# Thirty-six unread products in front, earlier weights, split runs of small products and a later modulation in a diffusion layer

## The chip, the cores and the metric

The kernel runs on one core of a Trainium2 chip. The metric is the device time of one execution in microseconds (us). Before the change three runs gave 960.75, 961.24 and 962.13 us; the median is 961.24 us.

## The reference

One layer of a hybrid diffusion model over 512 latent tokens and 256 context tokens, width 1024. All arithmetic is float32.

```python
mod = silu(c) @ w_ada + b_ada; mod_c = silu(c_ctx) @ w_ada + b_ada
sh1, sc1, gt1, sh2, sc2, gt2 = split(mod, 6)
h  = rms_norm(x, g_norm1) * (1 + sc1) + sh1
hc = rms_norm(ctx, g_norm1) * (1 + csc1) + csh1
aq, ak, av, dq, dk, dv, dz, da, db, ga, gd = split_cols(h @ w_in)      # and the same of hc
y_attn = window_ctx_attention(q_a, k_a, v_a, k_ac, v_ac, attn_sink)
o_dc, s_cf, s_cb = bidir_delta(context, zero states)    # chunks of 64 tokens, two directions
o_dl, _, _       = bidir_delta(latents, s_cf, s_cb)
y = sigmoid(ga) * (y_attn @ w_br_attn) + sigmoid(gd) * (y_d @ w_br_dn)
x = x + gt1 * (y @ w_out)
x = x + gt2 * (square(relu((rms_norm(x, g_norm2) * (1 + sc2) + sh2) @ w_mlp1)) @ w_mlp2)
```

The delta rule is computed in chunks of 64 tokens: in each chunk a triangular system is inverted, and a scan over the chunks carries a 64 x 64 state for each head and direction.

## The kernel before

**Layout.** Features lie on the 128 partitions and tokens on the free axis. Every large product is made as three passes of rounded float32: weights and activations are each split into a high and a low part (`hi`, `lo`), and `mm3` (L266 to L273) issues high x high (L271), high x low (L272) and low x high (L273). A weight block of 128 x 1024 (512 KB) is fetched by `wload` (L255 to L264): one DMA on the queue of SyncE into one of four buffers `wr`, then ACT writes the high part (L262) and VectorE (DVE) the low part (L263).

**Order.** The Python program writes the work in the order of priority. The framework then puts each engine's instructions into one fixed order from its own model of the times; on the chip each engine takes its own instructions in that order. Generators are woven by counts: `weave` advances several of them in proportion to step numbers, and `run_fill(n)` issues the next n of 432 products of 128 x 512 (L970 and L925: the attention branch's projection and the gate tiles) which serve as filling wherever a serial chain would leave TensorE (PE) waiting. `FILL` and the counts beside it set how many go where.

**Front (0 to 65 us).** SyncE issues x (four transfers of 512 KB), two blocks of `wada1`, the context (two transfers), then further blocks of `wada1`. `ada(kt)` (L190 to L201) multiplies the condition by its block of `w_ada` (L198), `columns(kt, ...)` (L209 to L222) turns the result into two columns of scale and shift (L212, L217, L220, L221). The sum of squares is built by ACT (L236) and DVE (L240, L244) and summed over partitions by a product with ones (L247). `modulate` (L275 to L279) makes the high and low part of one of eight blocks of h (L276, L277, L278). As each block becomes ready, three tiles of the input projection whose accumulators stay open in PSUM, the `early` ones, get that block's products: the decay and beta columns (`T_AB`) and the first two key tiles (`T_DK`, `T_DK + 1`). Their weights are loaded inside the loop over the blocks, two at block 0 and one at block 1.

**Middle (98 to 160 us).** `chunk_mats` (L687 to L726) builds the chunk matrices of three groups of four chunks. It begins with `half_products` (L675 to L685), one unbroken run of 128 small float32 products of 64 x 32 by 64 x 32; each takes two PE instructions of its own and two weight loads (256 matmuls and 256 loads in all, L684). It is woven with the attention's input tiles, 16 steps against 32. DVE then forms the matrices (L700, L712, L714, L721, L722), PE sums the decays (L701, L702).

**Late stage (376 to 433 us).** After the context's scan, `combine` (L768 to L800) forms the lower block of the inverse for each of the two latent groups: 64 small products (L776, L777), a copy by ACT (L778), 64 small products (L785, L786). Then, again for each group, `half_products` with q (L684), DVE multiplies with the decays (L1160, L1161) and ACT places the copies (L1168 to L1170). Ahead of each go `run_fill(28)` or `run_fill(36)` and `run_late(6)` or `run_late(3)`.

**Late modulation.** `late_mod` (L984 to L994) computes the remaining four groups of modulation columns without PE: for each of 32 blocks a DMA of 512 KB into a buffer of the same four `wr` buffers (L988), then one DVE instruction that multiplies and sums (L990). 24 of the 32 are issued by `run_late`; the last 8 are issued in the MLP.

**Second scan (431 to 511 us).** Eight steps of both directions, each step in three parts with a chain PE (L1036), DVE (L1040, L1041), PE (L1048), DVE (L1054), PE (L1067), DVE (L1078), and the outputs (L1085, L1090, L1093). Between the parts stand 8, 7 and 3 filling products. What is left of the 24 late blocks follows the scan.

**End.** The branch projection, the output projection (`mm3` with `residual`, L1253 and L1257, 24 products a tile), the norm, and the MLP.

## Time and profile before

The profile is of one execution on the chip. That execution took 959.5 us as the device counts it; its span, from the first instruction to the last, is 957.7 us.

| | |
|---|---|
| median of three runs | 961.24 us |
| profiled execution | 959.5 us |
| its span | 957.7 us |
| granted TensorE clock, mean | 0.979 |
| PE busy | 905.8 us, 95% |
| DVE busy | 596.6 us, 62% |
| ACT busy | 444.7 us, 46% |

PE is the matmul unit of TensorE, PEld its weight loads, DVE VectorE, ACT ScalarE, POOL GpSimd, SP SyncE (SPq is SyncE's queue, which issues the DMAs). The page gives busy times, the span in 40 slices (in tenths, with the granted PE clock in its own row), the DMA queues, the chain that ended last and the costliest groups of instructions. Further views are asked of the trace: waits (who waited for whom), windows (busy time, granted clock and DMA share in chosen stretches), lines (groups by source line) and a timeline. A busy PE is not a PE at its peak, because matmuls overlap; the spacing of starts says more.

### The profile page before, as it was taken

To read this page: it belongs to the slowest core of one execution; us is meant where nothing else is said; L and a number is where in the kernel's file an instruction comes from. 1 tells how busy PE (TensorE), PEld (TensorE's weight loads), DVE (VectorE), ACT (ScalarE), POOL (GpSimd) and SP (SyncE) were. 2 spreads that over 40 slices of the span, in tenths; PEclk is the share of its full clock that TensorE was granted. 3 is DMA by queue.
4 is the path that set the end of the run, shared out by engine and by line. 5 is a ranking of instruction groups with operands and counts; after the bars stand their busy time and mean duration, and the time that the engine had idled before them with its cause. 6 is when DMAs were issued, how large, how long until landed. Compare 5 with 4: busy or idle time off the path is not lost. (4 is left out here: it accounts for less than half of the span.)

```text
span 957.7 us, 18080 instructions
## 1 busy us (share of the span) xinstructions
PE 905.8 (95%) x7696; PEld 731.6 (76%) x7696; DVE 596.6 (62%) x994; ACT 444.7 (46%) x815; POOL 36.4 (4%) x45
## 2 busy tenths in 40 slices
PE   3999889999899999879999999999999999999998
PEld 1688667877677677658787879988888888888886
DVE  4666778997788899755577665982365225423511
ACT  5357634337567877337555433661154115313400
POOL 0001211000000000100011000000000000000000
PEclk9799989999999999889999999999999999999999
DMA  9721102110001133850123534381164213322101
GB/s 357 297 95 44 46 25 66 67 45 24 11 13 34 34 100 107 300 202 25 46 69 122 187 132 154 120 278 65 42 206 137 78 66 131 111 66 74 59 34 54
DMA packets 29601, 98.72 MB, mean 103 GB/s; under 512 B 3664, under 2 KB 4176, under 8 KB 29520
## 3 DMA queue, kind: packets, MB, share of 16 engines
q1 hardware_dynamic: 29520, 97.57, 29.6%
q8 instruction: 60, 0.98, 0.4%
q14 instruction: 21, 0.17, 0.0%
HBM read 95.46 MB, written 2.10 MB: 102 GB/s over the span
## 5 line engine op out<-in xcount | busy, mean ns | idle before, releaser
L271 PE MATMUL banks<-m,m 128*128 128x512 f32 (+1 forms) x584 | 219.8, 380 | 1.3 <-ACT m L277 1.3
L272 PE MATMUL banks<-m,m 128*128 128x512 f32 (+1 forms) x584 | 219.8, 378 | 0.0
L273 PE MATMUL banks<-m,m 128*128 128x512 f32 (+1 forms) x584 | 218.7, 378 | 0.8 <-DVE m L263 0.8
L262 ACT ACTIVATE m<-wr 128x1024 fp32r<-128x1024 f32 x67 | 71.1, 1062 | 149.8 <-PE banks L272 78.0
L271 PEld LDWEIGHTS banks<-m,m 128*128 128x128 f32 x584 | 109.7, 189 | 23.4 <-issue 3.1
L273 PEld LDWEIGHTS banks<-m,m 128*128 128x128 f32 x584 | 109.7, 189 | 22.0 <-DVE m L263 1.1
L272 PEld LDWEIGHTS banks<-m,m 128*128 128x128 f32 x584 | 110.1, 189 | 21.0 <-issue 0.8
L263 DVE TENSOR_TENSOR m<-wr,m 128x1024 fp32r<-128x1024 f32 x67 | 82.0, 1224 | 63.9 <-ACT m L262 34.8
L271 PE MATMUL banks<-m,wh 128*128 128x512 f32 (+1 forms) x312 | 114.3, 367 | 0.4 <-DVE m L537 0.4
L272 PE MATMUL banks<-m,wh 128*128 128x512 f32 (+1 forms) x312 | 112.2, 360 | 0.0
L273 PE MATMUL banks<-m,wl 128*128 128x512 f32 (+1 forms) x312 | 111.8, 359 | 0.0
L925 PE MATMUL banks<-m,wh 128*128 128x512 f32 x320 | 108.2, 413 | 0.0
L1352 DVE SCALAR_TENSOR_TENSOR m<-banks,modT,m 128x512 f32<-128x512 f32 x32 | 24.0, 750 | 104.0 <-PE banks L273 104.0
L262 ACT ACTIVATE wh<-wr 128x1024 fp32r<-128x1024 f32 (+1 forms) x60 | 56.6, 944 | 56.1 <-PE banks L272 23.9
L263 DVE TENSOR_TENSOR wl<-wr,wh 128x1024 fp32r<-128x1024 f32 (+1 forms) x60 | 64.7, 1078 | 22.6 <-ACT wh L262 22.3
L925 PEld LDWEIGHTS banks<-m,wh 128*128 128x128 f32 x320 | 61.7, 196 | 13.7
L925 PE MATMUL banks<-m,wl 128*128 128x512 f32 x160 | 67.3, 421 | 0.0
L271 PEld LDWEIGHTS banks<-m,wh 128*128 128x128 f32 x312 | 59.0, 189 | 9.5 <-DVE m L537 0.7
L272 PEld LDWEIGHTS banks<-m,wh 128*128 128x128 f32 x312 | 59.3, 190 | 9.0 <-issue 0.5
L273 PEld LDWEIGHTS banks<-m,wl 128*128 128x128 f32 x312 | 59.0, 189 | 8.7 <-DVE wl L263 0.3
L179 ACT ACTIVATE m<-m 128x512 fp32r<-128x512 f32 (+1 forms) x56 | 35.0, 630 | 47.5 <-DVE m L1335 19.9
L180 DVE TENSOR_TENSOR m<-m,m 128x512 fp32r<-128x512 f32 (+1 forms) x56 | 38.2, 689 | 20.9 <-ACT m L179 20.4
(229 smaller groups left out, 1293.3 us busy)
## 6 DMA issues: line engine op xcount, KB each, us to landing
wr<-in_wm SPq DMA_DIRECT2D x64, 512.0 KB, 3.5
wr<-in_win SPq DMA_DIRECT2D x39, 512.0 KB, 3.6
wa<-in_wada SPq DMA_DIRECT2D x32, 512.0 KB, 4.3
m<-in_wada SPq DMA_DIRECT2D x16, 512.0 KB, 10.2
m<-in_xT SPq DMA_DIRECT2D x8, 512.0 KB, 6.0
wr<-in_wbr SPq DMA_DIRECT2D x16, 256.0 KB, 2.7
wr<-in_wout SPq DMA_DIRECT2D x8, 512.0 KB, 3.7
out<-m SPq DMA_DIRECT2D x8, 256.0 KB, 2.0
```

Of the source, the lines that this page charges most:

```text
L179: A.activation(r32(hi), src, AF.Copy)
L180: (eng or V).tensor_tensor(r32(lo), src, hi, op=ALU.subtract)
L262: A.activation(r32(hi), raw, AF.Copy)
L263: V.tensor_tensor(r32(lo), raw, hi, op=ALU.subtract)
L271: PE.matmul(acc, w[0][:, k, :], xhi, start=(start and i == 0), stop=False)
L272: PE.matmul(acc, w[0][:, k, :], xlo, start=False, stop=False)
L273: PE.matmul(acc, w[1][:, k, :], xhi, start=False, stop=(stop and i == n - 1))
L925: PE.matmul(acc.ap, w[x][:, k, :], hx[k][y], start=(k == p == 0), stop=(k == KT - 1 and p == 2))
L1352: V.scalar_tensor_tensor(xn_[ct], acc.ap, modT[:, 3, ct:ct + 1], xn_[ct], op0=ALU.mult, op1=ALU.add)
```

## The change

1. 36 products of the 128 x 128 tile of ones with itself are issued on PE ahead of everything else; nothing reads them.
2. `wload` is defined earlier, and the three early weights are loaded one each: after the context's transfers, after block 1's `ada`, and in the first pass of the loop over blocks. The second key tile now takes part from block 0.
3. `half_products` yields after its first half. In the middle stage each half is followed by steps of the other work (`HPAUSE = 2`, the step count of the weave is 22 in place of 16). In the late stage 12 of the filling products that stood ahead of it are issued between the halves (`FPAUSE`). `combine` gets a call between its two runs, which issues 12 of the products that stood ahead of it (`CPAUSE`).
4. The 24 late blocks leave the late stage: one is issued after the second and one after the third part of each step of the second scan (16), the other 8 by twos in the first four tiles of the output projection.

```diff
+NONES = 36
 AHEAD = 2
-LATE = 6, 3, 0
+LATE = 1
+HPAUSE = 2
+FPAUSE, CPAUSE = 12, 12
...
+    wb_ = banks.get(512, True)
+    for _ in range(NONES):
+        PE.matmul(wb_[:, :P], ones, ones, start=True, stop=True)
+    wb_.free()
...
+    early, EARLY = [], {T_AB: 0, T_DK: 0, T_DK + 1: 0}
+    ebufs = []
+
+    def load_early():
+        bb = alloc(1024), alloc(1024)
+        ebufs.extend(bb)
+        early.append((wload(I["win"][list(EARLY)[len(early)]], bufs=bb), bank(2)))
+
     columns(0, ada(0))
     for k4 in range(KT // 4):
         nc.sync.dma_start(out=cs_[:, k4 * 1024:(k4 + 1) * 1024], in_=I["ctxT"][k4])
+    load_early()
...
-    early, EARLY = [], {T_AB: 0, T_DK: 0, T_DK + 1: 1}
-    ebufs = []
     for kt in range(1, AHEAD):
         columns(kt, ada(kt))
+        load_early()
...
-        for t_, k0 in EARLY.items():
-            if k0 == kt:
-                bb = alloc(1024), alloc(1024)
-                ebufs += bb
-                early.append((wload(I["win"][t_], bufs=bb), bank(2)))
+        if len(early) < len(EARLY):
+            load_early()
...
         for i in range(16):
+            if i == 8:
+                yield
...
-        half_products(kD, kO, gi, kT)
+        for _ in half_products(kD, kO, gi, kT):
+            for _ in range(HPAUSE):
+                yield
...
         A.activation(Ys.ap, Y.ap, AF.Copy)
         Y.free()
+        between()
         XO = bank()
...
-    weave((mats(), 16), (att, ATT))
+    weave((mats(), 16 + 3 * HPAUSE), (att, ATT))
...
-        run_fill(FILL[1])
-        run_late(LATE[0])
-        combine(NTO[1 + g], f[:, :, :HC], xr3[0][:, ms], b[:, :, :HC], xr3[1][:, ms], f, b, True)
+        run_fill(FILL[1] - CPAUSE)
+        combine(NTO[1 + g], f[:, :, :HC], xr3[0][:, ms], b[:, :, :HC], xr3[1][:, ms], f, b, True, lambda: run_fill(CPAUSE))
...
-        run_fill(FILL[2])
-        run_late(LATE[1])
+        run_fill(FILL[2] - FPAUSE)
         qD, qO = bank(), bank()
-        half_products(qD, qO, 1 + g, qT)
+        for _ in half_products(qD, qO, 1 + g, qT):
+            run_fill(FPAUSE)
...
         run_fill(FILL[3][n % 3])
-        if n % 3 == 2:
-            run_late(LATE[2])
+        if n % 3:
+            run_late(LATE)
     for _ in fill:
         pass
-    run_late(24)
...
         mm3(acc.ap, w, ys)
+        run_late(2)
         residual(ct, acc, slice(0, 512))
         acc.free()
+    run_late(24)
```

More of the change, by code (lines that the diff above doesn't have):

```diff
@@ L222, in columns, with wload @@
         mp_.free()
+    def wload(src, n=KT, bufs=None):
+        raw = sb.tile([P, KT, P], F32, tag="wr", bufs=NWR, name=nm("wr"))[:, :n]
+        nc.sync.dma_start(out=raw, in_=src)
+        if bufs:
+            hi, lo = (b.ap.rearrange("p (k c) -> p k c", k=KT) for b in bufs)
+        else:
+            hi, lo = (sb.tile([P, KT, P], F32, tag=t, bufs=NWS, name=nm(t))[:, :n] for t in ("wh", "wl"))
+        A.activation(r32(hi), raw, AF.Copy)
+        V.tensor_tensor(r32(lo), raw, hi, op=ALU.subtract)
+        return r32(hi), r32(lo)
+    early, EARLY = [], {T_AB: 0, T_DK: 0, T_DK + 1: 0}
[4 more added lines that the diff above has]
+        early.append((wload(I["win"][list(EARLY)[len(early)]], bufs=bb), bank(2)))
     columns(0, ada(0))
@@ L252, in tile_layer @@
         act(r, r, AF.Exp, scale=-0.5)
-    def wload(src, n=KT, bufs=None):
-        raw = sb.tile([P, KT, P], F32, tag="wr", bufs=NWR, name=nm("wr"))[:, :n]
-        nc.sync.dma_start(out=raw, in_=src)
-        if bufs:
-            hi, lo = (b.ap.rearrange("p (k c) -> p k c", k=KT) for b in bufs)
-        else:
-            hi, lo = (sb.tile([P, KT, P], F32, tag=t, bufs=NWS, name=nm(t))[:, :n] for t in ("wh", "wl"))
-        A.activation(r32(hi), raw, AF.Copy)
-        V.tensor_tensor(r32(lo), raw, hi, op=ALU.subtract)
-        return r32(hi), r32(lo)
     def mm3(acc, w, xs, start=True, stop=True, ks=None):
@@ L766, in back, with combine @@
         V.transpose(dst.rearrange("p m i -> p i m"), X3[g].rearrange("p r s -> p s r") if swap else X3[g])
-    def combine(nto, XTf, XRf, XTb, XRb, XAf, XAb, inplace):
+    def combine(nto, XTf, XRf, XTb, XRb, XAf, XAb, inplace, between=lambda: None):
         Y, Ys = bank(), alloc(512)
```

## The prediction

> **What bounds the kernel now.** I read the page first.

> ```profile
> span 957.7 us, 18080 instructions
> ...
> PE 905.8 (95%) x7696; PEld 731.6 (76%) x7696; DVE 596.6 (62%) x994; ACT 444.7 (46%) x815; POOL 36.4 (4%) x45
> ...
> DVE  4666778997788899755577665982365225423511
> ...
> PEclk9799989999999999889999999999999999999999
> ...
> q8 instruction: 60, 0.98, 0.4%
> ```

> PE bounds it: 95% busy, no other engine over 62%. In the row PEclk (40 slices of 24 us, tenths of the full clock) the granted clock drops in the second slice, in the sixth and in the seventeenth and eighteenth. So I asked the waits of PE, then a table of stretches (us; busy time and count of PE, PEld, DVE, ACT, POOL; granted clock; DMA share; GB/s).

> ```profile
> PE banks L684 <- issue: 11.3, 5, 3.4
> PE banks L198 <- DMA m<-in_wada: 11.1, 1, 11.1
> PE banks L785 <- issue: 3.6, 2, 2.0
> ...
> PE banks L1048 <- DVE m L1041: 0.9, 1, 0.9
> ```

> ```profile
> 11.10:20.10 9.00, 5.85 (x38) 1.89 (x38) 4.16 (x7) 3.61 (x6) 0.00 (x0) 1.00 1.03 411
> 20.10:33.70 13.60, 11.03 (x47) 7.01 (x48) 9.83 (x19) 6.60 (x12) 0.00 (x0) 0.50 1.03 410
> ...
> 98.30:136.40 38.10, 30.32 (x843) 22.41 (x841) 31.95 (x46) 20.04 (x35) 10.22 (x7) 0.91 0.13 44
> 380.70:431.00 50.30, 40.17 (x1127) 32.25 (x1126) 31.77 (x52) 18.95 (x29) 5.18 (x10) 0.85 0.72 252
> 441.80:451.60 9.80, 9.80 (x179) 8.03 (x178) 5.76 (x13) 6.64 (x27) 0.00 (x0) 1.00 0.16 57
> ```

> The longest waits of PE are for nothing that the profile shows (issue: 11.3 + 3.6 us), all in the runs of small products, and for the first block of `w_ada`. The clock is at 0.50 from 20 to 34 us, 0.91 in the middle and 0.85 in the late stage. The change touches just these stretches, and the second scan, where PE is full.

> **Front.** Twelve transfers of 512 KB stand ahead of the first early weight in SyncE's queue; with the change eight do. At 410 GB/s one takes 512 KB / 410 = 1.28 us, so it lands 5.1 us sooner; block 1 of `w_ada` lands 1.3 us later, block 2 2.6, block 3 1.3, the rest when they did. The rows are start, length, engine, line.

> ```profile
> 17.75 1.07 PE L198 MATMUL banks<-m,m 128*32 128x256 f32 x16 [0.57 <-DVE modS L221]
> 19.97 0.72 ACT L277 ACTIVATE m<-m,modS 128x512 fp32r<-128x512 f32 x1 [1.44 <-DVE m L276]
> 23.02 1.94 PE L198 MATMUL banks<-m,m 128*32 128x256 f32 x16
> 25.68 1.04 ACT L262 ACTIVATE m<-wr 128x1024 fp32r<-128x1024 f32 x1
> 26.77 0.79 PE L271 MATMUL banks<-m,m 128*128 128x512 f32 x1
> 64.68 0.40 PE L271 MATMUL banks<-m,wh 128*128 128x512 f32 x1
> ```

> ```profile
> L271 PE MATMUL banks<-m,m 128*128 128x512 f32 (+1 forms) x48 | 17.9, 377 | 0.0
> L198 PE MATMUL banks<-m,m 128*32 128x256 f32 x80 | 6.2, 412 | 0.0
> L217 PE MATMUL banks<-c_prm,m 128*128 128x2 f32 x21 | 2.9, 236 | 0.0
> ...
> 421.12 0.63 PE L925 MATMUL banks<-m,wh 128*128 128x512 f32 x2
> 421.81 0.63 PE L925 MATMUL banks<-m,wh 128*128 128x512 f32 x2
> ```

> Block 0's high part is there at 19.97 + 0.72 = 20.7 us, but the first early product starts at 26.77, behind the split of its weight (25.68 + 1.04). Three full products take 421.81 - 421.12 = 0.69 us, so 0.23 each, and one of half width is put at 0.117. From 26.77 to 64.68 PE does three lines of 48 (half of them full, half of half width: 72 x 0.23 + 72 x 0.117 = 25.0 us), five blocks of L198 (1.07 each at full clock: 5.4) and L217 (2.9): 33.3 us in 37.9. The rest is the 0.50 clock up to 33.7 and gaps.

> With the weight 5.1 us sooner the first early product can follow block 0's high part, at 20.0 (a little sooner than 20.7, as the same block of L198 takes 1.94 us at half clock and 1.07 at full). Block 2's `ada` is then still to do (1.6 us with L217). I add 2.5 us of gaps, since until 25 us weights and columns come one transfer at a time: 20.0 + 33.3 + 1.6 + 2.5 = 57.4, 7.3 us sooner, if the clock is granted from 20 us on. Two of its steps (3.4 us each) at half would cost 3.4. I take 6.5 us, range 3 to 9.

> ```profile
> 242.09 1.05 PE L536 MATMUL banks<-c_ident,st 128*128 128x128 f32 x8
> ```

> The 36 products cost nothing: four of their shape take 1.05 us, so 36 some 9 at full clock, 13 with the first 5 us at half; PE waits for `w_ada` until 11.1 us anyway. If they end at 12.5, the block's first products slip by 1.4 us, and the L247 behind them waits until 12.98 in any case. Their use is the clock. Before, it fell at 20.1 us though PE was busy 5.85 of the 9 us before, so the ones alone may not hold it to the first early product. [...] Hence 6.5, not 7.3.

> **Middle.**

> ```profile
> 100.27 1.67 PE L684 MATMUL banks<-m 64*32 64x32 f32 x175
> 104.03 0.73 PE L684 MATMUL banks<-m 64*32 64x32 f32 x61 [2.08 <-issue]
> 128.87 1.14 PE L684 MATMUL banks<-m 64*32 64x32 f32 x82 [2.38 <-DVE m L714]
> 416.13 1.05 PE L925 MATMUL banks<-m,wh 128*128 128x512 f32 x2
> 417.41 1.05 PE L925 MATMUL banks<-m,wh 128*128 128x512 f32 x2
> ```

> A run of 256 matmuls and 256 loads goes at about 9.5 ns a pair (1.67 / 175), then stops. The page has 60 instruction transfers of 0.98 MB in all, 16 KB each; 2 x 7696 PE instructions over 60 are 256 to a transfer. [...]

> ```profile
> L684 PE MATMUL banks<-m,m 64*32 64x32 f32 x512 | 5.5, 200 | 6.4 <-issue 6.4
> ...
> L925 PE MATMUL banks<-m,wh 128*128 128x512 f32 x68 | 24.9, 449 | 0.0
> L925 PE MATMUL banks<-m,wl 128*128 128x512 f32 x33 | 15.3, 464 | 0.0
> ```

> What a pause must be: these rows are of the late stage; its two unbroken runs of L684 stop for 6.4 us, 3.2 each. So a pause of some 3.2 us in the middle of a run hides its stop. The split puts about three attention steps of three products (0.69 us or more each) between the halves, 2.1 us, and a half itself is no longer than one block; I leave 0.3 us a run, up to 1.1. Issue stops here are 11.3 - 6.4 = 4.9 us. The clock at 0.91 of 38.1 us is 0.09 x 38.1 x 2 = 6.9 us at half, and the next step lies in the 136s: some three steps of 3.4 us. In one, three products take 417.41 - 416.13 = 1.28 us against 0.69, so a step loses 1.6; three lose about 4.1, as the middle one ran small products. Together 9.0 us.

> Not all of it comes back: DVE is busy 31.95 of 38.10 us here, so it becomes the bound once PE gains 6.2 us, and the 2.38 us wait for L714 with its clock step is DVE's already. [...] I take 5.5 us, range 2 to 9.

> **Late stage.** The stretch of 50.3 us holds 101 filling products (68 + 33 in the rows above, 23.2 us), four runs of `combine` of 128 pairs (9.5 ns each, 1.2 us), two of L684 (2.4 us) and eight changes of shape at 0.3: 35.2 us. The 15.1 us left are four stops (6.4 + 3.6 = 10.0) and the clock of 0.85, which by 0.15 x 50.3 is up to 7.5 us of lost clock, part of it under stops. The change moves no PE work out of this stretch; it puts 12 products (2.8 us, and 0.3 of switching) into each of the four places, 3.1 us against the 3.2 needed. I leave 0.3 a stop, 0.6 for two more switches and 0.5 for a chain that now shows: 15.1 - 1.2 - 0.6 - 0.5 = 12.8 us. [...] The removed 18 late blocks free DVE, for which PE did not wait here. Range 8 to 15.

> **Second scan and output projection.**

> ```profile
> DVE m L990 <- DMA wa<-in_wada: 11.4, 9, 4.0
> ...
> L990 DVE SCALAR_TENSOR_TENSOR m<-wa,m x32: 1214/1222/1496, 380.0 to 632.1; 128x1024 f32<-128x1024 f32 x32
> ...
> 442.11 1.23 DVE L263 TENSOR_TENSOR wl<-wr,wh 128x1024 fp32r<-128x1024 f32 x1 [0.20 <-ACT wh L262]
> 443.25 0.68 DVE L930 SCALAR_TENSOR_TENSOR m<-m,m 128x512 f32<-128x512 f32 x1
> 443.85 0.75 DVE L1040 TENSOR_TENSOR m<-banks,eg 128x256 f32<-128x256 f32 x2
> 445.86 1.15 PE L1048 MATMUL banks<-m,m 64*64 64x64 f32 x32
> ```

> A late block is put at 1.3 us of DVE (1222 ns and a short read of the sum). Two a step are 2.6 us in steps of 9.8 us, of which DVE works 5.76: 8.4, still under. Behind each waits the chain (L1040, L1054, L1078), and behind that PE with its next part. Here 1.9 us of L263 and L930 stood ahead of L1040, and L1048 still started in time. So a late block fits a gap as a rule; I put 0.1 us on each of 16, 1.6 us, and take back the one wait of L1048 for L1041 (0.9), which late blocks at the scan's end now cause: 0.7 lost. Bounds: 0.9 gained; 16 x 1.3 = 21 lost with no cover. The moved DMAs share SyncE's queue and the four `wr` buffers with the gate weights, 2 + 18/24 = 2.75 transfers a step on 4 buffers: over one step of lead. The other 8 blocks, two to a tile of 24 products (5.5 us), add 2.6 us to a DVE that the page has at 5 or 6 tenths in slices 24 and 25: just under full, and PE needs DVE only once a tile; 0, at most 3.

> **Sum.** 6.5 + 5.5 + 12.8 - 0.7 = 24.1 us off the execution of 959.5 us (span 957.7 and 1.8 around it). The median is 1.7 above that execution, so I forecast 961.2 - 24.1 = 937.1 us.

> **Rivals.**
> - A, the forecast, 0.64.
> - B, the front gives 1 us or nothing: ACT's fixed order still splits the first weight late, or block 1 and 2, now later, hold PE up. For it: DVE busy 9.83 of 13.60 us there. Against: the weight's split moves ahead in the program. 943 to 944 us; 0.15.
> - C, the stops are not a matter of fetched instructions, and halves change nothing (or the pauses are too short by far): front 6.5 less switches and scan, 957. [...] 0.07.
> - D, late blocks lie on the scan's chain without cover: 20 us given back, 956. Against: the 1.9 us above. 0.06.
> - E, slower: DVE meets late blocks whose transfer has not landed, as it did nine times for 11.4 us before (1.3 each, 4.0 at most), and everything behind waits. 16 x (1.3 + 1.3) = 41.6, less 25.7: 977 us. It decides from 1.6 us a block on. Against: one to 4.9 us here, where before nine waits came at one to 2 us. 0.05.
> - That nothing moves as written, or gains and losses cancel: 0.03.

> **The numbers.** B's 944 and the ends of A (3 + 2 + 8 less 3 of scan and projection: 951; 9 + 9 + 15 and 0.9: 927) give 927 to 951; C, D, E and the last lie outside, 0.2. Faster by over 0.2% (1.9 us, what a measurement tells here): A, B, C, D, 0.92; within: 0.03; slower: 0.05.

> **What would show it.** Right: PE busy from 1 us; clock 1.00 at 20 to 34 us; first early product near 20 us, first `wh` product near 58; issue waits of L684 and L785 under 3 us together; no 0.50 in the late stage, which shrinks from 50 to about 37 us; scan steps still under 10 us. Wrong: stops as long with a pause before them; L1048 or L1067 waiting for DVE by over 0.3 us a step; DVE waiting for `wa` in the scan.

## The result and the profile after

The changed kernel takes 948.87 us, the median of four runs (946.67, 946.76, 950.98 and 952.39), beside 961.0 us before. The ratio is 0.9875, with a 95% interval of 0.9837 to 0.9913. The gain is 12.1 us where 24.1 were forecast: inside the range, at half the size.

The profiled execution is the one of 950.98 us, with a span of 949.2 us. Its page first, then the waits of PE (us in total, times, longest).

```profile
span 949.2 us, 18234 instructions
...
PE 915.3 (96%) x7768; PEld 738.1 (78%) x7768; DVE 596.2 (63%) x994; ACT 444.6 (47%) x815; POOL 37.4 (4%) x45
...
PEclk8899999999999999999999999999999999999999
```

```profile
PE banks L394 <- ACT m L391: 4.1, 2, 2.4
PE banks L289 <- ACT m L240: 3.4, 1, 3.4
PE banks L700 <- issue: 3.0, 2, 2.0
...
PE banks L1055 <- issue: 2.2, 1, 2.2
```

The lines have moved: the half products are L700 (L684 before), `mm3` is L289 to L291, the first part of a scan step is L1055 (L1036), a late block L1009 (L990), the filling products L944 (L925), the split of a weight L240 and L241. The 11.1 us wait for `w_ada` is filled by the ones, which count as busy. The issue waits fell from 14.9 us to 5.2 (3.0 + 2.2), but one of them stands at a place where none stood, and ACT is new in the list.

The stretches that answer to those before (us; busy time and count of PE, PEld, DVE, ACT, POOL; granted clock; DMA share; GB/s), and the second scan of before for comparison:

```profile
15.51:18.93 3.42, 0.16 (x2) 0.07 (x1) 2.64 (x5) 3.42 (x5) 0.00 (x0) 1.00 1.02 406
18.93:32.58 13.65, 12.98 (x54) 6.33 (x54) 6.62 (x12) 5.00 (x10) 0.00 (x0) 0.50 1.03 410
96.40:136.40 40.00, 34.60 (x863) 25.63 (x861) 34.10 (x46) 20.84 (x36) 9.27 (x6) 0.91 0.14 42
378.70:417.50 38.80, 37.93 (x1137) 30.11 (x1136) 15.55 (x20) 23.32 (x40) 5.19 (x10) 1.00 0.29 91
417.50:500.40 82.90, 78.41 (x1397) 63.19 (x1389) 58.74 (x125) 48.13 (x154) 7.06 (x8) 1.00 0.41 129
```

```profile
431.00:510.30 79.30, 78.42 (x1395) 63.91 (x1389) 49.34 (x106) 50.06 (x162) 6.27 (x8) 0.99 0.19 61
```

The clock is at 0.50 for as long as before (13.65 us), only 1.1 us sooner. The late stage is what was hoped: 38.8 us in place of 50.3, without a stop and at full clock. The scan is 3.6 us longer with the same PE work.

All kernels are cut here at the same five places by the starts of PE's instructions (us): the first `wh` product, the first transpose of the attention's outputs, the first product of `combine` for the latent groups, the start of the second scan, its last output.

| kernel | to first `wh` | middle | outputs, first scan | late stage | second scan | rest | median | ratio to before, 95% |
|---|---|---|---|---|---|---|---|---|
| before | 64.7 | 135.0 | 181.0 | 50.3 | 79.3 | 447.4 | 961.0 | |
| changed | 64.6 | 131.9 | 182.1 | 38.8 | 82.9 | 448.8 | 948.9 | 0.9837 to 0.9913 |
| late_alone | 64.8 | 135.0 | 182.4 | 46.1 | 80.3 | 447.6 | 955.5 | 0.9938 to 0.9969 |
| blocks_back | 62.1 | 131.9 | 180.5 | 46.1 | 82.1 | 447.3 | 949.4 | 0.9869 to 0.9911 |
| no_pause | 63.6 | 132.0 | 182.3 | 42.1 | 84.9 | 449.2 | 956.0 | 0.9928 to 0.9971 |
| mid_whole | 64.5 | 130.9 | 177.9 | 38.7 | 84.7 | 448.5 | 948.5 | 0.9864 to 0.9903 |
| clock_held | 62.2 | 132.1 | 179.3 | 38.7 | 81.8 | 448.4 | 943.7 | 0.9808 to 0.9843 |
| mid_quarters | 62.1 | 137.8 | 178.7 | 38.7 | 81.1 | 447.9 | 948.5 | 0.9853 to 0.9901 |
| held_8_after_scan | 63.1 | 132.1 | 179.2 | 39.3 | 80.8 | 447.8 | 944.0 | 0.9804 to 0.9855 |
| no_ones | 62.8 | 132.9 | 177.7 | 39.9 | 83.0 | 449.1 | 944.3 | 0.9817 to 0.9871 |
| held_no_ones | 62.2 | 134.5 | 177.7 | 39.3 | 85.4 | 447.9 | 949.5 | 0.9866 to 0.9927 |
| held_more | 61.6 | 132.0 | 184.9 | 38.7 | 81.2 | 448.7 | 946.7 | 0.9830 to 0.9892 |
| ones_alone | 64.1 | 130.9 | 183.3 | 44.6 | 84.3 | 447.3 | 957.1 | 0.9944 to 0.9987 |
| shift40 | 63.6 | 132.0 | 178.0 | 39.0 | 81.2 | 449.5 | 945.1 | 0.9814 to 0.9870 |

Stretches are of one execution, medians of four to twelve. The column of the outputs and the first scan, which no kernel edits, varies from 177.7 to 184.9 us: a difference of that size is no effect of an edit by itself. The front varies too: PE's order up to the first `wh` product is one and the same in the changed kernel, blocks_back, no_pause and mid_whole, and that product comes at 64.6, 62.1, 63.6 and 64.5 us.

### The profile page after: what moved, and what is told of

Same layout as the page of the kernel before. It is cut to its first block, busy times and chain, and to the rows that moved or that the text cites. A ratio compares the mean times of both kernels' runs of the same rounds, so it can differ in the third digit from the quotient of the medians.

```text
span 949.2 us, 18234 instructions
## 1 busy us (share of the span) xinstructions
PE 915.3 (96%) x7768; PEld 738.1 (78%) x7768; DVE 596.2 (63%) x994; ACT 444.6 (47%) x815; POOL 37.4 (4%) x45
## 5 line engine op out<-in xcount | busy, mean ns | idle before, releaser
L289 PE MATMUL banks<-m,m 128*128 128x512 f32 (+1 forms) x584 | 220.3, 380 | 3.8 <-ACT m L240 3.4
L290 PE MATMUL banks<-m,m 128*128 128x512 f32 (+1 forms) x584 | 220.3, 379 | 0.2 <-DVE m L183 0.2
L291 PE MATMUL banks<-m,m 128*128 128x512 f32 (+1 forms) x584 | 220.1, 378 | 0.0
L240 ACT ACTIVATE m<-wr 128x1024 fp32r<-128x1024 f32 x67 | 70.9, 1062 | 153.9 <-PE banks L290 91.9
L289 PEld LDWEIGHTS banks<-m,m 128*128 128x128 f32 x584 | 109.8, 189 | 26.9 <-ACT m L240 3.4
L241 DVE TENSOR_TENSOR m<-wr,m 128x1024 fp32r<-128x1024 f32 x67 | 81.8, 1224 | 75.4 <-ACT m L240 39.3
L291 PEld LDWEIGHTS banks<-m,m 128*128 128x128 f32 x584 | 109.8, 189 | 21.9 <-issue 1.2
L289 PE MATMUL banks<-m,wh 128*128 128x512 f32 (+1 forms) x312 | 114.1, 367 | 1.3 <-DVE m L1270 0.8
L291 PE MATMUL banks<-m,wl 128*128 128x512 f32 (+1 forms) x312 | 112.2, 360 | 0.3 <-DVE wl L241 0.3
L944 PE MATMUL banks<-m,wh 128*128 128x512 f32 x320 | 105.4, 402 | 0.0
L241 DVE TENSOR_TENSOR wl<-wr,wh 128x1024 fp32r<-128x1024 f32 (+1 forms) x60 | 64.6, 1077 | 36.0 <-ACT wh L240 35.5
L240 ACT ACTIVATE wh<-wr 128x1024 fp32r<-128x1024 f32 (+1 forms) x60 | 56.5, 943 | 32.6 <-PE banks L290 17.6
L944 PEld LDWEIGHTS banks<-m,wh 128*128 128x128 f32 x320 | 59.3, 188 | 12.8
L289 PEld LDWEIGHTS banks<-m,wh 128*128 128x128 f32 x312 | 59.2, 190 | 10.9 <-DVE m L1270 1.0
L290 PEld LDWEIGHTS banks<-m,wh 128*128 128x128 f32 x312 | 59.3, 190 | 9.0 <-issue 0.5
L291 PEld LDWEIGHTS banks<-m,wl 128*128 128x128 f32 x312 | 59.1, 190 | 9.0 <-DVE wl L241 0.8
L944 PE MATMUL banks<-m,wl 128*128 128x512 f32 x160 | 65.6, 410 | 0.3 <-DVE wl L241 0.3
L182 ACT ACTIVATE m<-m 128x512 fp32r<-128x512 f32 (+1 forms) x56 | 35.2, 631 | 47.6 <-DVE m L1354 21.1
L183 DVE TENSOR_TENSOR m<-m,m 128x512 fp32r<-128x512 f32 (+1 forms) x56 | 38.4, 688 | 20.7 <-ACT m L182 20.2
```

The source lines that it names most:

```text
L182: A.activation(r32(hi), src, AF.Copy)
L183: (eng or V).tensor_tensor(r32(lo), src, hi, op=ALU.subtract)
L240: A.activation(r32(hi), raw, AF.Copy)
L241: V.tensor_tensor(r32(lo), raw, hi, op=ALU.subtract)
L289: PE.matmul(acc, w[0][:, k, :], xhi, start=(start and i == 0), stop=False)
L290: PE.matmul(acc, w[0][:, k, :], xlo, start=False, stop=False)
```

## The experiments

### The late stage: pauses, and blocks

**late_alone**: the kernel before with the late stage's pauses alone.

```diff
-        run_fill(FILL[1])
+        run_fill(FILL[1] - CPAUSE)
...
-        run_fill(FILL[2])
+        run_fill(FILL[2] - FPAUSE)
...
-        half_products(qD, qO, 1 + g, qT)
+        for _ in half_products(qD, qO, 1 + g, qT):
+            run_fill(FPAUSE)
```

> The kernel before with the late stage's pauses alone: the runs of combine and of the q products are cut in the middle by 12 filling products taken from those ahead of them; ones, early weights, middle and late modulation stay as before. Theory (the late stage's gain is fetched instructions hidden behind a pause): the stage between the first run of combine for the latent groups and the scan shrinks by 11 to 12 us as it did in the changed kernel (50.3 to 38.8), L684 and L785 lose their 10 us of issue waits there, and the median falls by 10 to 11 us, to 950 to 951, less about 2 us if the scan's first run now stops. Rival (the gain needs the late blocks gone from this stage): it stays above 44 us and the median above 955.

The stage took 46.1 us, the median was 955.5: the theory fell, the rival holds. The stops are nearly gone, but other waits stand in their place. The waits of late_alone from 382 to 428 us (its late block is L995, the weight's split L263, the copy in `combine` L782):

```profile
ACT wh L263 <- DMA wr<-in_win: 8.6, 2, 5.5
...
DVE m L995 <- DMA wa<-in_wada: 5.9, 6, 2.4
ACT m L782 <- DVE m L995: 3.2, 2, 1.8
...
PE banks L790 <- DVE modT L998: 1.8, 1, 1.8
...
PE banks L930 <- ACT wh L263: 1.6, 1, 1.6
```

And the issues of SyncE's queue there, and ACT's split behind them (start, length):

```profile
387.79 0.33 SPq L258 DMA_DIRECT2D wr<-in_win  x1
388.94 9.66 SPq L993 DMA_DIRECT2D wa<-in_wada  x5
```

```profile
394.78 1.06 ACT L263 ACTIVATE wh<-wr 128x1024 fp32r<-128x1024 f32 x1 [5.45 <-DMA wr<-in_win]
```

A late block seems to cost here in three ways. Its DMA stands in the queue among the transfers of the filling products' weights, and shares the four `wr` buffers with them: ACT waited 5.45 us for one weight. Its DVE instruction waits for that DMA. And the copy of `combine` (L782), on PE's chain, waited up to 1.8 us for a late block, though it reads nothing of it; it writes a buffer of the arena, in which each block takes and frees a scratch buffer of 1024 columns, which may be why. None of the three was tried alone.

**blocks_back**: the changed kernel with the late modulation where it was.

```diff
+        run_late(LATE[0])
...
+        run_late(LATE[1])
...
-        if n % 3:
-            run_late(LATE)
     for _ in fill:
         pass
+    run_late(24)
```

> The changed kernel with the late modulation where it was before (6 and 3 blocks in the late stage, the rest behind the second scan, 8 in the MLP). Theory (the blocks in the scan and in the output projection cost 1.4 us of DVE waits in the scan and 1.5 us behind it): the scan goes from 82.9 to about 81.5 us, with its first issue wait of 2.2 us still there, the late stage stays within 1 us of 38.8, the whole is 2 to 3 us faster than the changed kernel, 946 us. Rival (the blocks cost nothing, the scan lost to the issue wait alone): scan 82.9 as changed, same time within 1 us.

The late stage went to 46.1 us, 7.3 longer, which neither theory had. The scan is 0.8 us shorter, with its first stop still there (1.9 us), the rest 1.5. The median is the changed kernel's all the same (949.4 and 948.9). The profiled execution is 2.5 us shorter in front and 1.6 in the outputs, where nothing was edited; that all executions are is not shown, so what the blocks are worth to the whole stays open here, and the stage alone is counted.

**no_pause**: the changed kernel without the pauses of the late stage.

```diff
-FPAUSE, CPAUSE = 12, 12
+FPAUSE, CPAUSE = 0, 0
```

> The changed kernel without the pauses of the late stage (FPAUSE and CPAUSE 0), the late blocks still gone from it. With the kernel before (late stage 50.3 us), the pauses alone (46.1) and both (38.8) this is the fourth corner. Theory now: the late blocks held up the stage by themselves (late weights, and the copy of combine waiting for a DVE block), hidden before behind the stops; so here the stops come back, two of about 2 and two of about 3.3 us, and some clock steps with them, and the stage takes 47 to 50 us; the whole 7 to 10 us slower than the changed kernel, 956 to 959. Rival (the blocks were the larger cost by themselves, and the pauses do only 4 us): 42 to 44 us, 952 to 953.

The stage took 42.1 us (the rival's number), the whole 956.0 (the theory's), because stops moved on into the scan: in no_pause it began with one of 2.8 us. So late stage and scan are to be read together: 129.6 us before, 121.7 changed, 127.0 without the pauses, 128.2 with the blocks back. The fairer corner without either is not the kernel before but ones_alone (below): it too has the 36 products in front, which by themselves move stops (see "Where the stops stand"), and takes 128.9. Beside that, moving the blocks alone gains 1.9 us, the pauses alone 0.7, and both together 7.2. Each of the two parts is worth little without the other.

### The middle

**mid_whole**: the changed kernel with whole runs in the middle.

```diff
-HPAUSE = 2
+HPAUSE = 0
```

> The changed kernel with the middle's runs whole again and the weave at 16 steps. Theory (the halves gained nothing in the middle, as DVE or the order behind the weave is the limit there): the middle up to the first output of the attention takes 196.5 - 96.5 = 100 us as in the changed kernel, within 1.5 us, though issue waits come back to about 5 us from 3. Rival (the halves gained there and the chance of a clock step hid it): 3 us or more longer.

The middle was 1.0 us shorter, not longer, and the median the same (948.5). It had no clock step in the middle, though, where the changed kernel had two, so the halves' own worth is hidden behind that; no gain of theirs is shown. **mid_quarters** cuts the runs in four, in the kernel clock_held of the next section:

```diff
-            if i == 8:
+            if i in cuts:
...
-        for _ in half_products(kD, kO, gi, kT):
+        for _ in half_products(kD, kO, gi, kT, (4, 8, 12)):
...
-    weave((mats(), 16 + 3 * HPAUSE), (att, ATT))
+    weave((mats(), 16 + 9 * HPAUSE), (att, ATT))
```

> The kernel with the 10 further unread products (943.7 us), and the middle's runs cut in four parts in place of two, two steps of the other work behind each part. Theory (a block of 256 PE instructions takes 3.3 us to come; a half run can fill a block by itself, a quarter run can't): the stops of L708 in the middle go from 2.8 to under 1 us, and the stretch from the first half product to the first output of the attention from 100.1 to 97 to 98.5 us; the whole 1 to 3 us faster, 941 to 943. Rival (DVE, or ACT behind the attention's inputs, sets the pace in the middle): stops go, but the stretch stays at 99.5 to 101 us, and the time with it.

It lost 5.7 us in the middle and still had one stop of 2.4. The rival is nearer, and even too kind. Why the halves do so little is in the changed kernel's own timeline of PE (start, length; in brackets the idle time before):

```profile
111.94 0.40 PE L289 MATMUL banks<-m,wh 128*128 128x512 f32 x1
114.70 2.08 PE L394 MATMUL banks<-m,c_bones 128*128 128x512 f32 x2 [2.37 <-ACT m L391]
116.71 2.42 PE L700 MATMUL banks<-m 64*32 64x32 f32 x210
121.14 0.77 PE L700 MATMUL banks<-m 64*32 64x32 f32 x46 [2.01 <-issue]
```

The halves of the second group are not apart: the fixed order of PE has 210 and 46 products in one run, with a stop of 2.01 us in it, and the attention's step that could have stood between them stands ahead, with PE idle for 2.37 us behind ACT. A yield in a generator is a request; the order of PE has to be read.

### The front: what holds the clock

**clock_held**: the changed kernel with 10 more unread products, of ones by `rstd`, ordered behind block 0's columns.

```diff
         act(r, r, AF.Exp, scale=-0.5)
+        if r is rx:
+            unread(10)
...
+    def unread(n):
+        wb_ = banks.get(512, True)
+        for _ in range(n):
+            PE.matmul(wb_[:, :P], ones, rstd[:, :P], start=True, stop=True)
+        wb_.free()
```

> The changed kernel and 10 more unread products (ones by the inverse norm of x), which stand between the columns of block 0 and the first early product, where PE waited 3.36 us (15.67 to 19.03) and behind which the clock was 0.50 for 13.65 us. Theory (this wait lets the clock fall, and the front's gain goes with it): the clock stays at 1.00 for most of 19 to 33 us, the first wh product comes at 58 to 61 us in place of 64.6, and the whole is 4 to 6 us faster than the changed kernel, 943 to 945 us. Rival (the clock falls whatever fills the gap, or the order and the data set the pace): half clock after 19 us as before, first wh product at 64 to 66 us, no gain.

The whole took 943.7 us, as the theory said, but hardly for its reason. The clock held until 26.39 us, and yet the first `wh` product came at 62.2, short of the 58 to 61, and no sooner than in blocks_back (62.1). That one has the changed kernel's front, wait and all; its clock fell too, but only for 6.83 us (stretches of blocks_back):

```profile
14.37:17.79 3.42, 0.69 (x8) 0.52 (x4) 1.60 (x4) 3.42 (x6) 0.00 (x0) 1.00 1.03 412
17.79:24.61 6.82, 5.69 (x21) 1.74 (x21) 3.60 (x5) 1.55 (x3) 0.00 (x0) 0.50 1.03 408
```

And of the 5.2 us by which clock_held beats the changed kernel, shift40 (below) gets 3.7 without these 10 products, by the same number of added instructions; the intervals of those two ratios overlap. That holding the clock made the whole faster is not shown.

**held_more** adds 6 behind block 1's columns:

```diff
     for kt in range(1, AHEAD):
         columns(kt, ada(kt))
+        unread(6)
```

> The kernel with the 10 further unread products, and 6 more behind block 1's columns, in the stretch of 23.0 to 26.4 us that was 0.70 busy and was followed by 3.41 us at half clock. Theory (a stretch that is busy enough keeps the clock): full clock from 5 us on, first wh product 1 to 1.7 us sooner than 62.2, the whole 0.5 to 1.7 us faster than 943.7. Rival (the 6 products take 1.7 us of PE themselves, and PE is the bound by then): first wh product at 62 to 64 us, no gain.

The clock now never falls in front (stretches of held_more):

```profile
15.13:18.55 3.42, 2.56 (x21) 2.31 (x20) 2.72 (x5) 3.39 (x5) 0.00 (x0) 1.00 1.04 413
18.55:21.96 3.41, 3.33 (x19) 1.30 (x21) 2.49 (x4) 0.09 (x1) 0.00 (x0) 1.00 1.02 404
21.96:25.37 3.41, 2.34 (x21) 1.83 (x16) 1.77 (x5) 2.80 (x6) 0.00 (x0) 1.00 1.03 411
25.37:28.79 3.42, 3.42 (x32) 2.07 (x31) 2.28 (x4) 1.58 (x4) 0.00 (x0) 1.00 1.03 411
28.79:61.60 32.81, 32.81 (x235) 24.84 (x234) 21.15 (x44) 13.19 (x24) 0.78 (x2) 1.00 0.56 203
```

The first `wh` product comes at 61.6: with the full clock, and the 6 products' own 1.6 us of PE, the front gains 3.1 us on the kernel before, no more. The whole was 3 us slower than clock_held all the same (the intervals overlap). The profiled execution, the slowest of six, has a stop of 1.7 us in the outputs (220.3 us) and four stretches at half clock between 199 and 323 us, where that of clock_held has one.

**no_ones** and **held_no_ones** leave out the 36 products, without and with the 10; **ones_alone** puts the 36 into the kernel before.

```diff
-NONES = 36
+NONES = 0
```

> The changed kernel without the 36 products in front. Theory (they kept the clock only up to the wait at 15.7 to 19.0 us, and so bought nothing): first early product and first wh product within 1 us of the changed kernel's 19.0 and 64.6. The 144 PE instructions that go shift the borders of the blocks of 256 against the code; by the theory that a stop stands where such a border is reached under 3.3 us behind the one before, the border at PE instruction 8642 leaves the scan's first run, its stop of 2.2 us goes, and the scan takes 80 to 81 us in place of 82.9. The whole 0 to 3 us faster. Rival (the ones hold the clock and save in front): first wh product 2 us or more later, the whole slower.

> The changed kernel with the 10 unread products behind block 0's columns, but without the 36 in front. Theory (36 products raise the clock at 5 us, and nothing that PE has to do before 19 us is long enough to gain by it; what counts is that PE is busy enough in each stretch of 3.4 us from 12 us on): PE runs at half clock from 11 to about 22 us and at full clock from there, the first wh product comes at 61.5 to 63 us, and the whole is within 1.5 us of the kernel with both (943.7). Rival (the clock must be up before the early products, so that the 36 are needed): half clock to 28 us as without any unread product, first wh product at 62.8 us or later, 944.3 us or more.

> The kernel before with the 36 unread products in front and nothing else. Theory (the ones raise the clock early, but the stretch of 3.4 us behind block 0's columns was 0.47 busy, so the clock falls at about 20 us as before): half clock from 20 to 33 us, first wh product at 64 to 65 us as before (64.7), the front gains nothing; the late stage keeps its four stops within 2 us in sum, and the whole stays at 959 to 962. Rival (the ones are the part that gains in front): the clock holds past 20 us, first wh product at 61 to 63 us, 956 to 958.

Without the 36 the changed kernel takes 944.3 us (the intervals of the two ratios overlap), and reaches the first `wh` product at 62.8, within the 62.1 to 64.6 of the same front with them. Its theory missed in the scan, which took 83.0 us and not 80 to 81: a stop of 1.14 us stands there further on (419.0 us). Its PE at 26 to 29 us:

```profile
26.16 0.63 PE L290 MATMUL banks<-m,m 128*128 128x512 f32 x1
...
29.01 0.39 PE L290 MATMUL banks<-m,m 128*128 128x512 f32 x1
```

The product of 0.63 us is at half clock, that of 0.39 at full (a product of this line and shape takes 0.63 us at 28.60 in the changed kernel, where 0.50 is granted): the clock is up by 29.0 us, against 32.6 in the changed kernel and 24.6 in blocks_back. The 36 raised it at 5.3 us in the changed kernel (their records start 0.21 us apart up to there, 0.11 behind it), for work that PE did not yet have, and behind the wait of 3.36 us it was down again (0.50 from 18.93). With the 10 the front does not need the 36 either (62.2 with and without). ones_alone shows the same in the old order: half clock from 18.8 us for 13.65 us, first `wh` product at 64.1. Its whole was 3.7 us faster than before, the rival's number and not the theory's, but for neither's reason: places far from the front changed. The late stage took 44.6 us in place of 50.3, the scan 84.3 in place of 79.3, the middle 130.9 in place of 135.0. held_no_ones lost, 949.5, with a stop of 2.7 us in the scan's first run, where clock_held has none. What an edit in front has to do with a stop at 418 us is the next question.

### Where the stops stand

I numbered the records of PE and PEld, those of their sequencer included, in order of start. Every issue stop of over 0.6 us of every kernel, 47 in all, stands at a number of the form 194 + 256 k, or one less: 6594, 7106, 7874 and 8386 before; 8642 in the changed kernel, blocks_back, mid_whole and no_pause (2.0 to 2.8 us); 8642 again in held_no_ones, further on in the scan's first run; 4290 in held_more, in the outputs.

The traces also have the transfers that bring the instructions: packets of 16 KB on the queue q8, one to each border in order. Each of the 47 stops ends 1.25 to 1.62 us after its border's packet has landed. So a stop is a wait for instructions. Some of them (us):

| kernel | PE goes on at | stop | packet from, to |
|---|---|---|---|
| before | 413.90 | 3.37 | 411.70, 412.66 |
| before | 430.20 | 3.07 | 427.79, 428.94 |
| changed | 420.13 | 2.18 | 417.84, 418.77 |
| ones_alone | 426.84 | 3.50 | 424.45, 425.33 |
| shift40 (below), the changed kernel's border | 412.41 | none | 408.74, 409.97 |

At first I took it that from one border to the next a run of small products needs at least some 3.3 us (3.34 in the middle of the changed kernel, 3.35 before), and that a stop is what is missing to that; the next kernel was forecast by this rule. The 36 products are 144 records, and move all the code behind them by 144 places against the borders; the 10 of clock_held move it by 40, and there no stop stands in the scan. **shift40** does the shift alone: 10 of the 36 products become 20 of 64 columns. PE's time in front was to stay the same; in fact the product behind them started at 13.7 us in place of 11.3, and the first early product came 1.4 us later.

```diff
-NONES = 36
+NONES = 26
...
+    for _ in range(20):
+        PE.matmul(wb_[:, :64], ones, ones[:, :64], start=True, stop=True)
```

> The changed kernel with 10 of its 36 unread products cut into 20 of 64 columns, so that about the same PE time in front holds 40 PE instructions more; all else, the halves, the pauses and the late blocks too, is the changed kernel. Theory (a stop stands where a border of the instruction blocks of 256 is reached under some 3.3 us behind the border before it): the border that lay 17 PE instructions into the scan's first run now lies 23 ahead of it, in the last run of q products, and the block that ends there holds 24 filling products; the stop of 2.2 us at the scan's first run goes, the scan takes 80 to 81.5 us in place of 82.9 (without a clock step in it), the front stays (first wh product at 64 to 65 us), and the whole is 0.5 to 3 us faster than the changed kernel, unless another border falls badly. Rival (the stop hangs on the code there, the run of q products that passes into the scan without a pause, and not on the place of the border): the stop of 2 us or more stays at the scan's first run, the scan at 82.5 to 85 us.

The stop goes, as the theory said. The passage into the scan, of the changed kernel and of shift40 (its lines are 2 higher):

```profile
416.28 1.29 PE L700 MATMUL banks<-m,m 64*32 64x32 f32 x128
417.50 0.45 PE L1055 MATMUL banks<-m,m 64*64 64x64 f32 x8
420.13 1.85 PE L1055 MATMUL banks<-m,m 64*64 64x64 f32 x56 [2.18 <-issue]
```

```profile
411.43 1.29 PE L702 MATMUL banks<-m,m 64*32 64x32 f32 x128
412.65 2.08 PE L1057 MATMUL banks<-m,m 64*64 64x64 f32 x64
```

The same run passes into the same scan, without the stop, so the rival is out. The 3.3 us are not the rule, however: the border ahead of this one is reached 2.04 us behind the one before it (405.87 to 407.90) and PE does not stop, as its packet had landed at 405.25. That transfer ran ahead while a block with long work was on; what starts one I have not worked out.

The scan takes 81.2 us, the issue waits of the middle fell from 3.0 us to 1.5, and the whole is 945.1 us, 3.7 below the changed kernel (the intervals of the two ratios still overlap). Between the two profiled executions lie 5.8 us: the scan is 1.7 of them, and the outputs and the first scan, without a clock step in that of shift40, are 4.1, which as far as is shown is no effect of the shift.

### What is left of the late blocks

**held_8_after_scan** takes the 8 blocks out of the output projection of clock_held, and issues them behind the scan.

```diff
     for _ in fill:
         pass
+    run_late(24)
...
-        run_late(2)
         residual(ct, acc, slice(0, 512))
         acc.free()
-    run_late(24)
```

> The kernel with the 10 further unread products (943.7 us), and the 8 late blocks of the output projection's first tiles issued behind the second scan in its place. Theory (those 8 held the projection up by 1.2 to 1.5 us): the stretch from the scan's last output to the end goes from 448.5 to 447.2 us, the whole about 1.2 us faster, 942.5. Rival (they lie beside PE there too): unchanged within 0.4 us.

The rest went from 448.4 to 447.8 us, half of what was expected and no more than it varies between kernels with the same blocks in the same place (447.9 to 449.5), and the time stayed (944.0 and 943.7).

No version has a lower median than clock_held, 0.9825 of the kernel before, where the changed one has 0.9875; held_8_after_scan, no_ones and shift40 cannot be told from it.

## Why the prediction was right in sign and wrong in size

**Front, forecast -6.5, measured -0.1** at the first `wh` product, and -2.6 at best where another kernel has the same front (blocks_back). Two steps failed. "If the clock is granted from 20 us on": it was not. The first early product came at 19.03, as forecast (20.0), but behind a wait of 3.36 us for the split of its weight, and the stretch ahead of it, 15.51 to 18.93, was busy for 0.16 us of 3.42; the next four were at 0.50. The price of such steps was in the text (two of them, 3.4 us), with the warning that the ones alone might not hold the clock; the forecast then leaned to the side on which they do. And the sum lacked work: held_more, at full clock throughout, gains 3.1 us and not 7.3. From its first early product (18.6) to 61.6 are 43.0 us, where the sum had 37.4. Counted from each start to the next, the 144 early products took 28.1 us and not 25.0: they had been priced as one stream, and here they are mixed with the products of the columns. Block 1's `ada` and columns were still to do as well as block 2's (L213 and L232 below, of held_more; 1.7 us more than the sum has for both lines), and so was the context's sum of squares (L282, 0.6). The 6 products (L194) are 1.5, and the waits were 1.1 us, where 2.5 had been added for gaps. Together that is 5.5 of the 5.6.

```profile
19.37 0.64 PE L213 MATMUL banks<-m,m 128*32 128x256 f32 x8
...
20.50 0.62 PE L213 MATMUL banks<-m,m 128*32 128x256 f32 x2
21.13 0.70 PE L282 MATMUL banks<-m,ones 128*128 128x256 f32 x2
21.76 0.63 PE L213 MATMUL banks<-m,m 128*32 128x256 f32 x6
22.89 0.61 PE L232 MATMUL banks<-c_prm,m 128*128 128x2 f32 x4 [0.49 <-ACT m L227]
24.06 1.60 PE L194 MATMUL banks<-m,ones 128*128 128x128 f32 x12 [0.57 <-DVE modS L236]
```

In short, the mix of shapes was priced as a stream, and the work that was done before the early products had been left ahead of them in the sum, though these moved past it. Rival B gave this time for the front, and its reason, ACT's split as the last to come, is the wait of 3.36 us behind which the clock fell.

**Middle, forecast -5.5, measured -3.1** (135.0 to 131.9). Inside its range by luck, and not by the step given: whole runs gave -4.1, in an execution without a clock step there. Of three runs one stayed in one piece; stops went from 4.8 to 3.0 us and a wait for ACT came in place of the rest. The step that charged three clock steps to the stops took one execution for the rule: mid_whole has the same whole runs, stops of 5.2 us, and no step in the middle at all.

**Late stage, forecast -12.8, measured -11.5.** The size is nearly right, and the reason only half: "the removed 18 late blocks free DVE, for which PE did not wait here" was false as soon as the stops were gone. In the kernel before the pauses alone give -4.2; with the blocks back in the changed kernel, 7.3 of its 11.5 are lost. Some of the 11.5 is due to neither: ones_alone, with the stops moved and nothing else done here, takes 44.6. The lost clock did come back once the stops were gone (1.00 from 378.70 to 417.50), but a fall does not need a stop as long as those: in the changed kernel the clock fell behind 257.86 to 261.27, busy for 1.80 of 3.41 us, where the longest wait was 1.2. For its 0.3 us a change of shape the forecast gives no row, and no run shows it for a single change; the trace of before shows it for a round trip at full clock: the small products start 0.32 us behind the last large one, where large ones start 0.23 apart, the next large one 0.12 behind the last small one, where small ones start 0.01 apart, and the one after it 0.34 later (380.41 to 382.28). What a wait hides is not in the list of waits.

**Scan, forecast +0.7, measured +3.6.** PE's busy time is the same (78.4 us), so all of it is waiting. The stop is 2.2, at a border that the 144 records in front moved to the scan's first run (ones_alone stops there too, for 3.5 us). The other waits are 1.4 us longer, and those are the late blocks', where 1.6 had been put on them and 0.9 taken back; blocks_back shows only 0.8, as it ran 3.41 us of the scan at half clock. The count of 256 instructions to a transfer (the forecast's "block") was right, and used only for runs inside the late stage; counted on, the places of the borders were to be had. How many such blocks PE holds at a time no run shows. 3 of the changed kernel's 60 borders show a stop of over 0.6 us; in and behind runs of small products a border cost up to 3.5 us (ones_alone).

**Output projection, forecast 0, at most 3; measured +1.4**. Moving its 8 blocks away gave back 0.6, which is within what this stretch varies by itself.

**What no step had**: three clock steps between 200 and 323 us in the profiled execution. Between the first transpose of the attention's outputs and the late stage it takes 182.1 us, and mid_whole, without a step there, 177.9 (the kernel before has none there either and takes 181.0, which stays open). Their waits are old. The wait of 2.4 us for DVE stands in both kernels, up to 205.12 us before and up to 201.96 after. The stretches of 3.41 us around it, before and after:

```profile
200.96:204.37 3.41, 1.80 (x10) 1.05 (x8) 3.41 (x6) 0.07 (x1) 0.00 (x0) 1.00 0.00 0
204.37:207.78 3.41, 2.66 (x14) 2.05 (x15) 3.41 (x8) 0.47 (x1) 0.00 (x0) 1.00 0.00 0
```

```profile
199.83:203.25 3.42, 1.29 (x6) 0.95 (x7) 3.42 (x7) 0.00 (x0) 0.00 (x0) 1.00 0.00 0
203.25:206.66 3.41, 3.41 (x12) 2.62 (x11) 2.46 (x9) 0.87 (x3) 0.00 (x0) 0.50 0.48 141
```

Before, the wait lies across the edge of two stretches, busy for 1.80 and 2.66 us, and the clock stays at 1.00; after, it lies almost wholly within one, busy for 1.29, and the next runs at half clock. The edges lie elsewhere from profile to profile: with one and the same order of PE in front the clock fell at 18.93 us in the changed kernel and at 17.79 in blocks_back. That fits the spread of the changed kernel's four runs: mean clock 0.990 and 0.993 in the two of 946.7 us, 0.983 and 0.981 in those of 951.0 and 952.4. Here a single profile can be off by some 5 us from the next.

## What to carry to other kernels

A step that is moved forward moves past work, which has to be added to what follows it. Products of mixed shapes are not priced as one stream (28.1 us here, where a stream gave 25.0). A gain that needs the clock is checked stretch by stretch up to the work, most of all at the last wait ahead of it: here 36 early products did not hold it over a stretch busy for 0.16 of 3.42 us, and in held_more, with no stretch from 15.13 us on under 2.34 of 3.41, it held, though in clock_held it fell behind one of 2.38. Where runs of small instructions stop for nothing, number the instruction records and look for equal distances (256 here). Mixing the runs with long work then helped in the late stage (issue stops of 10.0 us before, none in the changed kernel), and every edit ahead that adds instructions, an unread product too, moves the borders (36 products by 144 places here), and with them stops of up to 3.5 us that have nothing to do with it. So before an edit is credited with a few us, shift the code alone, and see how far the same code varies. When a stop is taken out, ask what it hid, and change one part alone beside the whole before crediting either.
